# A layer of block products on one core: three of seven products accumulated on one PSUM bank, with half weight units and another order at the turns

## The chip, the cores and the metric

One Trainium2 chip, one core. The metric is device time in microseconds of one execution. The kernel before takes 1847.15 us in the median of three runs (1845.55 to 1848.17).

## What is computed

One layer of a decoder trunk with two gated feed-forward networks and a mixing stage between them, over 1072 tokens (16 meta tokens, 1024 of a prompt, 32 new ones) of width 1024; a feed-forward network has 2816 inner channels.

```python
def rmsnorm(x, g):
    y = xf * lax.rsqrt(jnp.mean(xf * xf, axis=-1, keepdims=True) + EPS)
    return (y * g)
def swiglu(x, wg, wu, wd):
    return (jax.nn.silu(x @ wg) * (x @ wu)) @ wd

x = x + 0.5 * swiglu(rmsnorm(x, g1), w1g, w1u, w1d)
h = rmsnorm(x, gm)
z = h @ w_in + b_in
u = z[..., :C] * sigmoid(z[..., C:2*C])          # then causal conv of width 31, LayerNorm, silu -> c
p_in = z[..., 2*C:]                               # then trailing means over 2/4/8/16 tokens, linear map -> q
x = x + concat([c, q]) @ w_out + b_out
x = x + 0.5 * swiglu(rmsnorm(x, g2), w2g, w2u, w2d)
y = rmsnorm(x, gf)
```

Everything is float32. The outputs are y for prompt and new tokens and the last inputs of convolution and pooling.

## The kernel before, in words

**Numbers and pieces.** Each float32 operand is split into a high part (a cast, by ScalarE, L140) and a low part (source minus high part, L141, by VectorE, or by GpSimd for weights); a product is then three matmuls per 128 input channels: high by high, high by low, low by high (`mul`, L126 to L137; the matmul itself is L123). The tokens stand in three pieces X1, X2, X3 of 358 columns (the first two are padded a little), with channels on the partitions: X1 and X2 go through the first feed-forward network together (the first fast pass), X3 alone (the plain pass); in the second network X1 goes alone and X2 with X3.

**Weights.** A unit is 128 output channels by 1024 input channels or the like, 512 KB. `take` (L159 to L163) gives a loaded unit and issues the load of later ones on SP's queue, into `wraw` with four buffers. `half_unit` (L165 to L169) turns half a unit into `wh` and `wl`, six buffers each.

**Fast passes.** For two pieces, a block of 256 output channels by 1024 input channels is a 2 x 2 product of quarters and is computed with seven products m1 to m7 instead of eight (`block_steps`, L489 to L523). Each product has twelve matmuls of 358 columns and an accumulation bank of its own. VectorE makes four sums of weight quarters per block (L505 to L508). The operands (b11, b21, t1, t2, t3, t4, b22) are made ahead from the two normed pieces. `fast_pair` (L527 to L564) adds the products up: u1 = m1 (a ScalarE copy, L557), u1 + m2, u1 + m6, + m7, + m5 and so on, seven VectorE additions a block, all at L535. The results go to `sink`: a silu by ScalarE and a product by VectorE for the gate and up blocks, and casts and splits for the hidden operands (`group_sink`, L643 to L684; there `hid`, `dt1`, `dt4`, `db22`, `xb`, `cc` are hidden operands, their differences and scratch for them). A block pair p stands in the order gate block, down product of an earlier pair, up block. Four groups of pairs make up a pass; at a group's end the down products of a whole group follow.

**Order.** Matmuls keep the order in which the program emits them. On the other engines a scheduler orders instructions by its own estimates, so how the new program runs on an engine is not told by the diff alone. Background tasks (generators: norms, operands, the mixing stage) are stepped in a queue between the products, and `yield LAG` makes a task wait for that much matmul work (358/2400 a matmul).

**The start** (`Start`, L309 to L427). The first pair's products are made plainly, as the blocks of normed operands aren't there: eight products (c, j), c the piece, j over two gate and two up units, with the norm applied to the results. `norms(c)` makes reciprocal square roots: VectorE iterates, then multiplies an identity by them (`diag`, L206), and TensorE spreads them by a matmul on `ones`; ScalarE copies the result to `nr` (L215).

**Turns.** `to_second_piece` closes the first fast pass, launches `h1b` (the normed X3, split into `smt`) and finishes it. `to_last` launches `s2` (`fast_operands`, L271 to L307: square sums of X2 and X3, then for four k the seven operands of the second fast pass).

## Time and profile before

| | us |
|---|---|
| median of three runs | 1847.15 |
| the profiled execution | 1845.23 |
| its span, first to last instruction | 1843.5 |
| TensorE busy | 1747.4 (95%) |
| VectorE (DVE) busy | 1400.9 (76%) |
| GpSimd (POOL) busy | 1154.1 (63%) |
| ScalarE (ACT) busy | 761.2 (41%) |

The mean granted TensorE clock is 0.973 of full speed. The page's chain of work that ended last is TensorE's for 72% of the span and DVE's for 18%. PE is TensorE's matmuls, SP the engine that issues the loads. "x" counts instructions; a group is one line, engine and operation with its operands.

### The profile page before, as it was taken

To read this page: it belongs to the slowest core of one execution; us is meant where nothing else is said; L and a number is where in the kernel's file an instruction comes from. 1 tells how busy PE (TensorE), PEld (TensorE's weight loads), DVE (VectorE), ACT (ScalarE), POOL (GpSimd) and SP (SyncE) were. 2 spreads that over 40 slices of the span, in tenths; PEclk is the share of its full clock that TensorE was granted. 3 is DMA by queue.
4 is the path that set the end of the run, shared out by engine and by line. 5 is a ranking of instruction groups with operands and counts; after the bars stand their busy time and mean duration, and the time that the engine had idled before them with its cause. 6 is when DMAs were issued, how large, how long until landed. Compare 5 with 4: busy or idle time off the path is not lost.

```text
span 1843.5 us, 29182 instructions
## 1 busy us (share of the span) xinstructions
PE 1747.4 (95%) x10486; PEld 1726.9 (94%) x10486; DVE 1400.9 (76%) x2621; ACT 761.2 (41%) x1482; POOL 1154.1 (63%) x894
## 2 busy tenths in 40 slices
PE   8699999999899999999999999999799999999997
PEld 7699999999799999999999999999699899989997
DVE  8979797989746696898235888537878888797965
ACT  6434444444424324434235433535453434434344
POOL 6576766667635336667246658665577676766683
PEclk9799999999999999999999999999899999999998
DMA  6022222222243223343224493443233222222222
GB/s 204 24 74 78 78 69 69 79 73 95 97 91 119 76 70 101 129 135 118 69 93 136 120 139 127 137 137 120 87 92 94 74 70 69 82 77 72 69 92 87
DMA packets 74560, 176.17 MB, mean 96 GB/s; under 512 B 23728, under 2 KB 30128, under 8 KB 74416
## 3 DMA queue, kind: packets, MB, share of 16 engines
q1 hardware_dynamic: 74416, 174.31, 31.3%
q8 instruction: 83, 1.36, 0.3%
q14 instruction: 61, 0.50, 0.1%
HBM read 169.13 MB, written 5.15 MB: 95 GB/s over the span
## 4 chain that ended last, share of the span: by engine, by line
PE 72%; DVE 18%; issue 5%; DMA 3%; POOL 2%; ACT 1%; SPq 0%; DVEq 0%; POOLq 0%; ACTq 0%
PE acc L123 72%; DMA wraw<-in_wf 3%; POOL wl L141 2%; DVE acc L245 2%; DVE acc L535 1%; DVE wraw L506 1%; DVE tmp L535 1%; DVE acc L779 1%; DVE tmp L245 1%; DVE tmp L657 1%; DVE wraw L507 1%; DVE sx L505 0%; DVE x L456 0%; DVE dt4l L141 0%; DVE xk L245 0%
## 5 line engine op out<-in xcount | busy, mean ns | idle before, releaser
L141 POOL TENSOR_TENSOR wl<-wraw,wh 128x512 fp32r<-128x512 f32 x740 | 996.3, 1358 | 598.2 <-ACT wh L140 567.6
L140 ACT CAST wh<-wraw 128x512 fp32r<-128x512 f32 x740 | 453.9, 620 | 687.9 <-PE acc L123 465.6
L123 PE MATMUL acc<-smt,wh 128*128 128x358 f32 x1024 | 252.8, 328 | 4.5 <-DVE mixl L141 2.2
L123 PEld LDWEIGHTS acc<-smt,wh 128*128 128x128 f32 x1024 | 181.8, 190 | 5.8 <-DVE mixl L141 2.5
L779 DVE SCALAR_TENSOR_TENSOR acc<-ub,vecs,acc 128x340 f32<-128x340 f32 (+2 forms) x348 | 183.7, 573 | 2.7
L123 PE MATMUL acc<-mixlt,wh 128*128 128x340 f32 x704 | 167.0, 321 | 4.9 <-DVE smt L141 2.4
L123 PE MATMUL acc<-smt,wl 128*128 128x358 f32 x512 | 167.8, 328 | 0.0
L456 DVE SCALAR_TENSOR_TENSOR x<-acc,x 128x358 f32<-128x358 f32 (+1 forms) x240 | 119.5, 518 | 38.8 <-PE acc L123 38.1
L583 DVE SCALAR_TENSOR_TENSOR x<-acc,x 128x358 f32<-128x358 f32 x320 | 144.9, 518 | 0.2 <-PE acc L123 0.2
L123 PEld LDWEIGHTS acc<-mixlt,wh 128*128 128x128 f32 x704 | 121.9, 190 | 6.0 <-DVE smt L141 2.7
L535 DVE TENSOR_TENSOR acc<-tmp,acc 128x358 f32<-128x358 f32 x168 | 85.3, 527 | 51.3 <-PE acc L123 45.8
L141 POOL TENSOR_TENSOR wl<-sx,wh 128x512 fp32r<-128x512 f32 x58 | 86.0, 1484 | 49.1 <-ACT wh L140 46.8
L123 PE MATMUL acc<-mixlt,wl 128*128 128x340 f32 x352 | 112.8, 320 | 0.8 <-POOL wl L141 0.8
L123 PEld LDWEIGHTS acc<-smt,wl 128*128 128x128 f32 x512 | 96.9, 189 | 0.0
L505 DVE TENSOR_TENSOR sx<-wraw 128x512 f32<-128x512 f32 x58 | 62.4, 1076 | 38.5 <-DMA wraw<-in_wf 38.3
L507 DVE TENSOR_TENSOR wraw<-sx,wraw 128x512 f32<-128x512 f32 x58 | 78.7, 1357 | 9.8 <-POOL wl L141 9.7
L123 PE MATMUL acc<-mixh,wh 128*128 128x356 f32 (+1 forms) x320 | 79.9, 330 | 4.7 <-DVE mixl L141 2.7
L123 PE MATMUL acc<-mixl,wh 128*128 128x356 f32 (+1 forms) x320 | 79.1, 329 | 0.0
L123 PE MATMUL acc<-mixh,wl 128*128 128x356 f32 (+1 forms) x320 | 79.0, 329 | 0.0
L123 PE MATMUL acc<-xb,wh 128*128 128x358 f32 x256 | 65.9, 339 | 13.6 <-DVE tmp L535 9.6
L535 DVE TENSOR_TENSOR tmp<-tmp,acc 128x358 f32<-128x358 f32 x126 | 65.4, 519 | 13.2 <-PE acc L123 11.4
L482 DVE TENSOR_TENSOR acc<-acc,tmp 128x358 f32<-128x358 f32 (+1 forms) x44 | 23.2, 526 | 64.6 <-PE acc L123 51.2
(284 smaller groups left out, 4873.5 us busy)
## 6 DMA issues: line engine op xcount, KB each, us to landing
wraw<-in_wf SPq DMA_DIRECT2D x239, 512.0 KB, 3.3
wraw<-in_wf SPq DMA_DIRECT2D x66, 256.0 KB, 3.1
wraw<-in_win SPq DMA_DIRECT2D x24, 512.0 KB, 3.3
wraw<-in_wout SPq DMA_DIRECT2D x16, 512.0 KB, 3.3
x<-in_xt SPq DMA_DIRECT2D x8, 179.0 KB, 5.2
x<-in_xt SPq DMA_DIRECT2D x1, 1432.0 KB, 8.5
x<-in_xt SPq DMA_DIRECT2D x8, 178.0 KB, 4.6
out_yt<-tmp SPq DMA_DIRECT2D x8, 170.0 KB, 2.6
```

The lines of the kernel that those rows point to most:

```text
L123: tc.keep_in_program_order(nc.tensor.matmul(acc, lhs, rhs, start=start, stop=stop))
L140: nc.scalar.copy(hi, src)
L141: (engine or nc.vector).tensor_tensor(lo, src, hi, ALU.subtract)
L245: nc.vector.scalar_tensor_tensor(t, X(k, piece), col(gain, k), r, ALU.mult, ALU.mult)
L456: nc.vector.scalar_tensor_tensor(X(m, piece), acc, 0.5, X(m, piece), ALU.mult, ALU.add)
L482: nc.vector.tensor_tensor(acc, acc, box["s"], ALU.mult)
L505: nc.vector.tensor_tensor(s1, r1[:, :KH], r1[:, KH:], ALU.add)
L506: nc.vector.tensor_tensor(r1[:, :KH], r0[:, :KH], r1[:, :KH], ALU.subtract)
L507: nc.vector.tensor_tensor(r0[:, :KH], s1, r0[:, :KH], ALU.subtract)
L535: nc.vector.tensor_tensor(t, s, acc, ALU.add)
L583: nc.vector.scalar_tensor_tensor(to, acc, 0.5 * sign, to, ALU.mult, ALU.add)
L779: nc.vector.scalar_tensor_tensor(to, src, w, part, ALU.mult, ALU.add)
```

## The change

Five edits go together.

1. `chained` takes the place of `product` in 40 of 42 blocks: M6, M7 and M4 accumulate on M1's bank, in the order m1, m2, m6, m5, m7, m3, m4. After M1, M6 and M7 ScalarE copies the bank's state to `tmp` (km1, km6, km7); VectorE adds four times a block. The first pair after the start (`loose`) keeps the old form.
2. Weights come in half units: `wraw` tiles of 256 KB, eight of them, five loaded ahead.
3. X3's square sum is taken in the middle of the first fast pass from a copy that is loaded again into `tmp`, piece by piece.
4. `h1b` isn't finished at once, and the last pair's down product stands ahead of the plain pass; X2's norm for the second fast pass is launched with the mixing stage, and `fast_operands` makes its operands in another order, with one accumulation bank and three `tmp`.
5. The start makes the second norm after product (1, 0), and reads norms from the accumulation bank where it read them from `nr`; `outputs` writes to the products' own banks.

```diff
+LAG5 = 20.0
+LAG6 = 4.0
...
-R_BUFS = 4
+R_BUFS = 8
+AHEAD = 5
...
-        tc.keep_in_program_order(nc.tensor.matmul(acc, lhs, rhs, start=start, stop=stop))
+    def matmul(acc, lhs, rhs, start, stop, more=False):
+        tc.keep_in_program_order(nc.tensor.matmul(acc, lhs, rhs, start=start, stop=stop, skip_group_check=more))
...
-        return const.tile([P, KD, P], F32, name="wraw", tag="wraw", bufs=R_BUFS)
+        return const.tile([P, KH, P], F32, name="wraw", tag="wraw", bufs=R_BUFS)
...
-        fetch(2)
+        fetch(AHEAD)
...
+    def early_rms(piece, out):
+        a, b = piece
+        s = const.tile([P, N], F32, name="ns", tag="ns")[:, : b - a]
+        part = accum()[:, : b - a]
+        for k in range(KD):
+            t = temp()[:, : b - a]
+            nc.sync.dma_start(t, xt[:, k, a - PAD : b - PAD])
+            yield
+            if k == 0:
+                nc.scalar.activation(part, t, AF.Square)
+            else:
+                nc.scalar.activation(t, t, AF.Square)
+                nc.vector.tensor_tensor(s if k == KD - 1 else part, part, t, ALU.add)
+            yield
+        yield LAG5
+        out[piece] = yield from rsqrt(s, 1.0 / D, EPS, lag=LAG5)
...
-        yield from rms(p0, st)
-        yield from rms(p1, st)
+        for piece in pieces:
+            if piece not in st:
+                yield from rms(piece, st)
+        sub = nc.vector.tensor_tensor
         for k in range(KH):
-            b11, b21, b12, b22, t3 = (temp()[:, :n] for _ in range(5))
+            b11, b22, b21 = (temp()[:, :n] for _ in range(3))
+            t = accum()[:, :n]
             scaled(b11, p0, k, gain, st[p0])
+            scaled(b22, p1, KH + k, gain, st[p1])
+            yield
+            put("b11", k, b11)
+            put("b22", k, b22)
+            yield
+            scaled(t, p1, k, gain, st[p1])
+            t3 = temp()[:, :n]
+            sub(t3, b22, t, ALU.subtract)
+            sub(t, t, b11, ALU.subtract)
+            yield
+            put("t1", k, t)
+            put("t3", k, t3)
             scaled(b21, p0, KH + k, gain, st[p0])
             yield
-            put("b11", k, b11)
+            sub(t, b22, t, ALU.subtract)
+            put("t2", k, t)
             put("b21", k, b21)
             yield
-            scaled(b12, p1, k, gain, st[p1])
-            scaled(b22, p1, KH + k, gain, st[p1])
-            yield
-            nc.vector.tensor_tensor(t3, b22, b12, ALU.subtract)
-            nc.vector.tensor_tensor(b12, b12, b11, ALU.subtract)
-            yield
-            put("t1", k, b12)
-            put("t3", k, t3)
-            put("b22", k, b22)
-            yield
-            nc.vector.tensor_tensor(b22, b22, b12, ALU.subtract)
-            put("t2", k, b22)
-            yield
-            nc.vector.tensor_tensor(b21, b21, b22, ALU.subtract)
-            put("t4", k, b21)
-            yield
+            sub(t, b21, t, ALU.subtract)
+            put("t4", k, t)
+            yield LAG6
...
-                self.outputs(0)
+                self.norms(1)
+                self.gate(0)
+                self.outputs(0, 0)
+                self.outputs(0, 1)
                 self.first_blocks()
             elif (c, j) == (1, 0):
                 self.norms(1)
-            elif (c, j) == (1, 2):
-                self.norms(1)
+            elif (c, j) == (1, 1):
+                self.gate(1)
                 self.differences()
-            elif (c, j) == (1, 3):
-                self.outputs(1)
-                self.last_blocks()
-                rest_of_start()
-        def outputs(self, c):
+            elif c == 1:
+                self.outputs(1, j - 2)
+                if j == 3:
+                    self.last_blocks()
+                    rest_of_start()
...
+        def gate(self, c):
             r = self.st[c]
             for i in range(2):
-                t = pools["fast"].tile([P, self.n], F32, name="cc", tag="cc", bufs=4)
+                t = self.gates[i] = pools["fast"].tile([P, self.n], F32, name="cc", tag="cc", bufs=4)
                 nc.vector.tensor_tensor(t, self.accs[c, "g", i], r, ALU.mult)
                 nc.scalar.activation(t, t, AF.Silu)
-                nc.vector.tensor_tensor(t, t, r, ALU.mult)
-                nc.vector.tensor_tensor(t, self.accs[c, "u", i], t, ALU.mult)
-                if i not in self.hid:
-                    fa1_places(0)
-                split(self.hid[i][0][c], self.hid[i][1][c], t)
+                nc.vector.tensor_tensor(t, t, self.inbank[c], ALU.mult)
+        def outputs(self, c, i):
+            acc = self.accs[c, "u", i]
+            nc.vector.tensor_tensor(acc, acc, self.gates[i], ALU.mult)
+            if i not in self.hid:
+                fa1_places(0)
+            split(self.hid[i][0][c], self.hid[i][1][c], acc)
...
+        def kept(acc):
+            t = temp()[:, :n]
+            nc.scalar.copy(t, acc)
+            return t
+        def chained(name, w):
+            ops = get()[OPERAND_OF[name]]
+            on = name in ("m6", "m7", "m4")
+            acc = st["m1"] if on else accum()[:, :n]
+            block_product(acc, w, ops, not on)
+            if name in ("m1", "m6", "m7"):
+                st["m1"], st["k" + name] = acc, kept(acc)
+            elif name == "m2":
+                sink(0, 0, add(st["km1"], acc, acc))
+            elif name == "m5":
+                st["m5"] = acc
+            elif name == "m4":
+                sink(1, 0, acc)
+            else:
+                sink(0, 1, add(st["u4"], acc, acc))
+            if name == "m7":
+                st["u4"] = add(st["km6"], st["m5"], st["km6"])
+                sink(1, 1, add(st["km7"], st["m5"], st["m5"]))
...
-        return block_steps(src0, src1, product)
+        return block_steps(src0, src1, product if loose else chained)
...
+    CHAINED = ("m12", "m6", "m5", "m7", "m3", "m4")
...
-                put_blocks(g)
+                put_blocks(g, CHAINED)
...
+            elif p == 4 and first:
+                do(launch, "r1b", early_rms(FFN1_B, r1b))
...
-        launch("r1b", rms(FFN1_B, r1b))
...
-        finish("h1b")
     do(to_second_piece)
     put_down(fa1_d[PAIRS - 2])
+    put_down(fa1_d[PAIRS - 1])
     def to_first_mixing():
         close_pool("fast")
@@ -1129,7 +1197,7 @@
         open_pool("low", "right")
         open_mix()
-    plain_pass(fb1, fb1_d, fa1_d[PAIRS - 1], {
+    plain_pass(fb1, fb1_d, [], {
...
+        launch("s2", fast_operands(FFN2_B, "g2", box["s2"], r2b))
...
+            lambda: do(launch, "r2", rms(FFN2_B[0], r2b))],
```

In the order of instructions of each engine, three places change most. (New line numbers: L144 and L145 are the cast and the split L140 and L141; L576 the copy; L601 the addition L535; L266 is L245; L490 is L456; L516 is L482; a number behind a name tells apart tiles.)

ScalarE at the end of the first group of the first fast pass: before,

```order
L140 CAST wh<-wraw 128x512
L140 CAST hid1h<-acc 128x358
L140 CAST wh<-wraw 128x512
L140 CAST db22h_1404<-acc 128x358
L140 CAST wh<-wraw 128x512
L140 CAST dt4h_1448<-cc 128x358
L140 CAST hid2l<-tmp 128x358
L140 CAST wh<-wraw 128x512
L140 CAST hid0h<-acc 128x358
L557 COPY tmp<-acc 128x358
L140 CAST wh<-wraw 128x512
```

and now,

```order
L144 CAST wh<-wraw 128x512
L144 CAST xb<-cc 128x358
L144 CAST wh<-wraw 128x512
L144 CAST hid1h<-acc 128x358
L144 CAST hid0h<-acc 128x358
L144 CAST wh<-wraw 128x512
L576 COPY tmp<-acc 128x358
L144 CAST dt4h_1486<-cc 128x358
L144 CAST dt4h_1487<-cc 128x358
L727 ACTIVATE cc<-acc 128x358
L144 CAST wh<-wraw 128x512
L576 COPY tmp<-acc 128x358
```

The copy of M1 of the next block (the first L576 row; L557 before) stands in both behind the two `hid` casts of the finished group; now it has M6 of its block behind it, and the next two copies follow.

VectorE at the turn to the plain pass, where `smt` is made from X3: before,

```order
L141 TENSOR_TENSOR hid2l<-acc,hid2h 128x358
L637 TENSOR_TENSOR acc<-acc,cc 128x358
L245 SCALAR_TENSOR_TENSOR acc<-x_4804,vecs,nr 128x358
L141 TENSOR_TENSOR smt<-acc,smt 128x358 x4
L245 SCALAR_TENSOR_TENSOR acc<-x_4804,vecs,nr 128x358
L141 TENSOR_TENSOR hid1l<-acc,hid1h 128x358
L141 TENSOR_TENSOR smt<-acc,smt 128x358
L245 SCALAR_TENSOR_TENSOR acc<-x_4804,vecs,nr 128x358
L141 TENSOR_TENSOR db22l_5206<-acc,db22h_5204 128x358
L141 TENSOR_TENSOR smt<-acc,smt 128x358 x3
L456 SCALAR_TENSOR_TENSOR x_61<-acc,x_61 128x358
L456 SCALAR_TENSOR_TENSOR x_62<-acc,x_62 128x358
```

and now,

```order
L490 SCALAR_TENSOR_TENSOR x_61<-acc,x_61 128x358
L490 SCALAR_TENSOR_TENSOR x_62<-acc,x_62 128x358
L266 SCALAR_TENSOR_TENSOR acc<-x_4948,vecs,nr 128x358 x2
L490 SCALAR_TENSOR_TENSOR x_61<-acc,x_61 128x358
L490 SCALAR_TENSOR_TENSOR x_62<-acc,x_62 128x358
L266 SCALAR_TENSOR_TENSOR acc<-x_4948,vecs,nr 128x358
L145 TENSOR_TENSOR smt<-acc,smt 128x358 x2
L266 SCALAR_TENSOR_TENSOR acc<-x_4948,vecs,nr 128x358
L490 SCALAR_TENSOR_TENSOR x_61<-acc,x_61 128x358
L490 SCALAR_TENSOR_TENSOR x_62<-acc,x_62 128x358
L266 SCALAR_TENSOR_TENSOR acc<-x_4948,vecs,nr 128x358
L145 TENSOR_TENSOR smt<-acc,smt 128x358
```

The products of X3 by its norm (L245, now L266) and the `smt` splits ran in one piece; now the additions of the down product to x (L490) stand between.

VectorE at the turn to the second fast pass, from the diagonal (`diag`) on: before,

```order
L141 TENSOR_TENSOR b11l<-tmp,b11h 128x358
L141 TENSOR_TENSOR b21l<-tmp,b21h 128x358
L295 TENSOR_TENSOR tmp<-tmp 128x358
L141 TENSOR_TENSOR b22l<-tmp,b22h 128x358
L296 TENSOR_TENSOR tmp<-tmp 128x358
L482 TENSOR_TENSOR acc<-acc,tmp 128x340
L141 TENSOR_TENSOR t3l<-tmp,t3h 128x358
L302 TENSOR_TENSOR tmp<-tmp 128x358
L245 SCALAR_TENSOR_TENSOR tmp<-x_62,vecs,nr 128x358 x2
L141 TENSOR_TENSOR t1l<-tmp,t1h 128x358
L245 SCALAR_TENSOR_TENSOR tmp<-x_4804,vecs,nr 128x358
L141 TENSOR_TENSOR hid0l<-acc,hid0h 128x340
```

and now,

```order
L266 SCALAR_TENSOR_TENSOR tmp<-x_62,vecs,nr 128x358
L145 TENSOR_TENSOR b11l<-tmp,b11h 128x358
L516 TENSOR_TENSOR acc<-acc,tmp 128x340
L145 TENSOR_TENSOR hid1l<-acc,hid1h 128x340
L266 SCALAR_TENSOR_TENSOR tmp<-x_4948,vecs,nr 128x358
L266 SCALAR_TENSOR_TENSOR acc<-x_4948,vecs,nr 128x358 x2
L319 TENSOR_TENSOR tmp<-tmp,acc 128x358
L145 TENSOR_TENSOR b22l<-tmp,b22h 128x358
L320 TENSOR_TENSOR acc<-acc,tmp 128x358
L266 SCALAR_TENSOR_TENSOR tmp<-x_62,vecs,nr 128x358
L145 TENSOR_TENSOR t3l<-tmp,t3h 128x358
L145 TENSOR_TENSOR t1l<-acc,t1h 128x358
```

A `hid` split of the plain pass comes after three operations of the operands' making instead of after some fifteen, and t1's and t2's source is an `acc` tile in place of a `tmp`.

## Rows read from the trace of the kernel before

**Rows 1.** The page: span, and each engine's busy time.

```profile
span 1843.5 us, 29182 instructions
PE 1747.4 (95%) x10486; PEld 1726.9 (94%) x10486; DVE 1400.9 (76%) x2621; ACT 761.2 (41%) x1482; POOL 1154.1 (63%) x894
```

**Rows 2.** Table by stretch: start:end length, busy time of each engine, PEclk, DMA share, GB/s.

```profile
0.00:125.00 125.00, 100.23 (x537) 95.93 (x538) 104.82 (x181) 62.24 (x127) 81.99 (x69) 0.89 0.32 106
125.00:450.00 325.00, 317.38 (x1890) 314.06 (x1889) 286.24 (x477) 132.50 (x255) 219.53 (x161) 0.98 0.23 76
480.00:525.00 45.00, 38.81 (x223) 38.36 (x222) 27.56 (x51) 14.99 (x31) 18.48 (x14) 0.92 0.22 71
1262.00:1345.00 83.00, 68.29 (x416) 66.46 (x416) 67.93 (x113) 37.12 (x76) 43.26 (x31) 0.92 0.26 89
1440.00:1800.00 360.00, 349.96 (x2086) 344.83 (x2085) 308.42 (x515) 148.12 (x284) 247.68 (x183) 0.99 0.24 78
```

**Rows 3.** The same table for a stretch at full clock and for the first 35 us.

```profile
350.00:400.00 50.00, 50.00 (x306) 50.00 (x305) 39.59 (x70) 19.83 (x37) 35.66 (x26) 1.00 0.25 83
0.00:35.00 35.00, 29.24 (x148) 26.70 (x149) 26.26 (x54) 26.75 (x54) 19.63 (x20) 0.90 0.73 243
```

**Rows 4.** TensorE's waits (total, times, longest), 125 to 475 and 1345 to 1800.

```profile
PE acc L123 <- DVE tmp L535: 6.0, 6, 1.4
PE acc L123 <- DVE ns L235: 2.1, 1, 2.1
...
PE acc L123 <- DVE tmp L535: 6.6, 8, 1.4
```

**Rows 5.** Timeline around one group end: DVE and PE (start, duration, [idle before]).

```profile
1439.24 1.70 DVE L141 TENSOR_TENSOR xb<-cc,xb 128x358 fp32r<-128x358 f32 x1 [0.56 <-ACT xb L140]
...
1461.75 0.60 PE L123 MATMUL acc<-xb,wh 128*128 128x358 f32 x2 [0.45 <-DVE cc L681]
1464.00 0.59 PE L123 MATMUL acc<-xb,wh 128*128 128x358 f32 x2 [0.99 <-ACT cc L661]
1466.65 0.60 PE L123 MATMUL acc<-xb,wh 128*128 128x358 f32 x2 [1.42 <-DVE tmp L535]
1468.39 0.44 PE L123 MATMUL acc<-hid0h,wh 128*128 128x358 f32 x1 [0.48 <-DVE tmp L535]
```

**Rows 6.** Additions and weight casts (the page's groups) and the copy L557 (its line).

```profile
L140 ACT CAST wh<-wraw 128x512 fp32r<-128x512 f32 x740 | 453.9, 620 | 687.9 <-PE acc L123 465.6
L535 DVE TENSOR_TENSOR acc<-tmp,acc 128x358 f32<-128x358 f32 x168 | 85.3, 527 | 51.3 <-PE acc L123 45.8
L535 DVE TENSOR_TENSOR tmp<-tmp,acc 128x358 f32<-128x358 f32 x126 | 65.4, 519 | 13.2 <-PE acc L123 11.4
...
L557 ACT COPY tmp<-acc x42: 448/459/483, 71.7 to 1783.8; 128x358 f32<-128x358 f32 x42
```

**Rows 7.** Timeline at the turn to the plain pass: DVE and PE.

```profile
492.87 5.74 DVE L245 SCALAR_TENSOR_TENSOR acc<-x,vecs,nr 128x358 f32<-128x358 f32 x5
...
504.47 1.11 PE L123 MATMUL acc<-dt1h,wh 128*128 128x358 f32 x2 [6.19 <-DVE smt L141]
```

**Rows 8.** Timeline at the turn to the second fast pass: DVE and PE.

```profile
1314.50 1.59 DVE L141 TENSOR_TENSOR t4l<-tmp,t4h 128x358 fp32r<-128x358 f32 x1
...
1318.70 0.65 PE L123 MATMUL acc<-hid2h,wh 128*128 128x340 f32 x1 [10.18 <-ACT hid2h L140]
1321.11 0.65 PE L123 MATMUL acc<-hid2l,wh 128*128 128x340 f32 x1 [1.75 <-DVE hid2l L141]
...
1322.89 0.50 DVE L456 SCALAR_TENSOR_TENSOR x<-acc,x 128x340 f32<-128x340 f32 x1
```

**Rows 9.** Timeline of the start: PE.

```profile
51.55 1.65 PE L123 MATMUL acc<-diag,ones 128*128 128x128 f32 x6 [7.74 <-DVE diag L206]
...
66.45 0.67 PE L123 MATMUL acc<-b11h,wh 128*128 128x358 f32 x1 [6.07 <-DVE cc L383]
```

**Rows 10.** The page's DMA issues of weights: KB each, median us to landing.

```profile
wraw<-in_wf SPq DMA_DIRECT2D x239, 512.0 KB, 3.3
wraw<-in_wf SPq DMA_DIRECT2D x66, 256.0 KB, 3.1
wraw<-in_win SPq DMA_DIRECT2D x24, 512.0 KB, 3.3
wraw<-in_wout SPq DMA_DIRECT2D x16, 512.0 KB, 3.3
```

More of the change, by code (lines that the diff above doesn't have):

```diff
@@ L135, in mul @@
                     moving = rhs[c] if isinstance(rhs, list) else rhs[:, at : at + n]
-                    matmul(acc, lhs, moving, start and i == 0 and j == 0, stop and i == last and j == 2)
+                    matmul(acc, lhs, moving, start and i == 0 and j == 0, stop and i == last and j == 2,
+                           more)
                     at += n
@@ L169, in half_unit, with unit @@
         return wh, wl
-    def unit(raw):
-        return half_unit(raw[:, :KH]), half_unit(raw[:, KH:])
+    def unit():
+        return half_unit(take()), half_unit(take())
     def both_parts(w, k):
@@ L182, in blocks, with rsqrt @@
         return [min(at, n - P) for at in range(0, n, P)]
-    def rsqrt(src, scale, add, out=None, copied=True):
+    def rsqrt(src, scale, add, out=None, copied=True, lag=LAG2):
         n = src.shape[-1]
@@ L347, in norms @@
             if c not in self.steps:
-                self.steps[c] = rsqrt(self.sums[c], 1.0 / D, EPS)
+                self.steps[c] = rsqrt(self.sums[c], 1.0 / D, EPS, self.out[c])
                 next(self.steps[c])
@@ L351, in norms @@
                 self.st[c] = whole(self.steps[c])
+                self.inbank[c] = self.out[c]["psum"]
         def after(self, c, j):
@@ L456, in use @@
                         nc.vector.scalar_tensor_tensor(X(m, piece), acc, 0.5, X(m, piece), ALU.mult, ALU.add)
-            out.append(("step", [source], lambda: unit(take()), use, False))
+            out.append(("step", [source], lambda: unit(), use, False))
         return out
     def plain(src, use):
-        return ("step", [[(0, src)]], lambda: unit(take()), use, False)
+        return ("step", [[(0, src)]], lambda: unit(), use, False)
     def plain_ffn(wsrc, piece, get):
@@ L493, in make0 @@
         def make0():
-            st["r0"] = take()
-            return unit(st["r0"])
+            st["r0"] = take(), take()
+            return tuple(half_unit(r) for r in st["r0"])
         def use0(w):
@@ L553, in product @@
             ops = get()[OPERAND_OF[name]]
-            mul([acc], [(w[0][:, k], w[1][:, k], ops[0][:, k], ops[1][:, k]) for k in range(KH)])
+            block_product(acc, w, ops)
             if name == "m1":
@@ L593, in twist, with fast_ffn @@
             yield
-    def fast_ffn(wsrc, pieces, free, get, hid):
+    def fast_ffn(wsrc, pieces, free, get, hid, loose):
         n = N
@@ L1210, in use @@
                     between(m)
-        return ("step", raws, lambda: (unit(take()), unit(take())), use, False)
+        return ("step", raws, lambda: (unit(), unit()), use, False)
     def between(m):
@@ L1230, in trunk @@
     for p in steps:
-        raw_list.extend(p[1])
-    raw_list[0] = [(at, raw_list[0][0][1][:, at * P : (at + KH) * P]) for at in (0, KH)]
+        for _, src in sum(p[1], []):
+            raw_list.extend(src[:, at : at + KH * P] for at in range(0, src.shape[-1], KH * P))
     nc.sync.dma_start(vecs, vec)
     start.load(0, 0)
-    fetch(1)
+    fetch(2)
     for k in range(1, KD):
         start.load(0, k)
-    fetch(2)
+    fetch(4)
     for k in range(KD):
```

56 lines of the change are left out of this document (28 added, 28 removed).

## The prediction

> **What bounds the kernel now.** The first view is the page's list of engines: TensorE works 95% of the span, and it is the only engine near full; ScalarE works 41% of it [rows 1]. So a change pays only where it removes TensorE's losses. The second view is the table by stretch, from which I read two losses: the time in which TensorE does nothing (length less PE busy) and the time in which it works at less than the full granted clock ((1 - PEclk) x length). In 125 to 450 these are 7.6 + 6.5 = 14.1 us, in 1440 to 1800 they are 10.0 + 3.6 = 13.6 us, in 480 to 525 6.2 + 3.6 = 9.8 us, and in 1262 to 1345 14.7 + 6.6 = 21.3 us [rows 2]. The first two stretches are the two fast passes (blocks in seven products), the third is the turn from the first fast pass to the plain pass, the fourth the turn from the plain pass to the second fast pass. At full clock 306 matmuls take 50.00 us, so a matmul takes 163 ns and a product of twelve 1.96 us [rows 3]; that is the unit in which I measure every delay below.
>
> The third view tells what TensorE waits for. In the fast stretches nearly all of it is the DVE addition at L535: 6.0 us in 6 waits in the first, 6.6 us in 8 in the second; one wait of 2.1 us on the sum of squares of X3 (`ns`) comes beside them [rows 4]. The timeline of one group end shows how: four waits of 0.45, 0.99, 1.42 and 0.48 us, 3.3 us together, follow each other, while DVE works without a gap [rows 5].
>
> **The chained blocks.** Forty blocks give up three of seven additions each (7 in `settle` and `product`; 4 in `chained`): 120 operations of 0.53 us [rows 6] that start 0.44 us apart, some 53 us of DVE work. TensorE does no more and no fewer matmuls. DVE is not the bound on average, so this is worth only what it moves in the group ends. There two blocks stand behind each other, so 6 x 0.44 = 2.6 us of the 3.3 us of wait go. If the 12.6 us of waits on L535 go, and with them their share of the clock loss (12.6 of 17.6 us idle, so 7.2 of 10.1 us), it is 19.8 us; the half units and the freed banks (4 instead of 7 per block) can add a little and the stretching of DVE's operations beside GpSimd's, such as the 1.70 us of an `xb` split [rows 5], can take some back. I take **-18 us**; bounds -5 (only the longest wait of each group end shortens) and -25.
>
> Against it stand the new copies. M6 may not write on M1's bank before ScalarE has copied it, M7 not before the copy of M6, M4 not before that of M7. A copy takes 0.46 us and a cast 0.62 us [rows 6]. In the new order of ScalarE (first place shown above) one weight cast stands ahead of most copies. With six operand buffers, that cast (six products ahead) waits for the buffer which the product to be copied has just freed, so the copy is there about 0.62 + 0.46 = 1.08 us after its product's end, and another product of 1.96 us lies between (M2, M5, M3): no wait. At the eight group ends the order is worse: the copy of the first M1 stands behind both `hid` casts, which wait for some ten DVE operations after M3 of the group, and behind a cast for which M2 must have ended. So M6 waits at least 1.08 us from M2's end, more where one of those operations is stretched. I take 1.4 us, **+11 us** for eight; bounds 0 (the new stall only takes the place of the old ones) and +28 (3.5 us each: two splits stretched from 0.53 to 1.70 us on top of 1.08).
>
> **X3's statistics early.** They are computed in the middle of the pass from a copy read again, instead of at its end. The wait of 2.1 us [rows 4] goes: **-2 us** (0 to -4 with the clock). The price is eight more transfers on SP's queue that wait for a free `tmp` and have weight loads behind them; five half units are ahead there, 5 x 1.96 = 9.8 us of cover. If the cover were gone, the next thing late would be a weight cast; bound +4 us.
>
> **h1b interleaved.** Before, the whole second operand is made ahead of two downs: TensorE stands 6.19 us for `smt` splits, because the banks of those norms are held while DVE works off five L245 of 1.15 us and the splits [rows 7]. In the new order (second place) the 96 matmuls of each down, 15.7 us at 163 ns, lie between, and DVE alternates between L490 and L266. The 6.19 us go, and part of the 3.6 us of clock: **-8 us** of 9.8; bounds -4 and -9.8. What is late next is an `smt` split at the plain pass's first unit.
>
> **s2 shortened.** At the last turn TensorE waits 10.18 us for `hid2h` and 1.75 us for `hid2l`, since ScalarE and DVE work first through the fast operands of the second pass; a split of two SBUF operands took 1.59 us there, an operation with one PSUM operand 0.50 us [rows 8]. The change gives t1, t2 and t4 a PSUM tile, which makes about half of its 60 operations of the second kind; it takes X2's square sum out of this place; and it sets a pause of 4 units of the program's clock (358/2400 a matmul, so 27 matmuls) between the four k, so that `hid` operations come sooner (third place). Sixty operations lose some 30 x 0.5 = 15 us of DVE time, more than the 11.9 us of waits. **-16 us** of the stretch's 21.3; bounds -8 (only the clock and the small wait) and -20.
>
> **Start.** The second norm's diagonal is now awaited one product of each kind earlier. Before, TensorE waits 7.74 us for it and 6.07 us for the gate product [rows 9]. Two products of 24 matmuls, 7.8 us at 163 ns, move behind the first wait: it gets longer by up to that, and the second has that much more cover. **0 us**; bounds -6 (the second wait gone) and +8 (nothing won back).
>
> **Half units.** Transfers of 256 KB took 3.1 us where those of 512 KB took 3.3 us [rows 10]; the count of weight transfers goes from 345 to 624. In the first 35 us, where all queues are loaded, 243 GB/s were moved [rows 3], more than one transfer at a time gives (256 KB in 3.1 us are 85 GB/s), so transfers overlap, and the 71 to 106 GB/s of the stretches [rows 2] are below it. Nothing for itself: **0 us** (their use is in the -18); bounds 0 and the rival below. The Trainium skill, "DMA: Bandwidth & Descriptors", section Bandwidth, speaks against this edit: transfers should be gathered to 1 MiB or more, and 64 KB ones reach only 32% of the peak. By that rule the edit costs time where loads are the bound (rival 5). The trace agrees that the fixed part is most of a transfer (3.1 us against 3.3 us for twice the bytes).
>
> **Sum**, against the profiled execution's 1845.2 us (its span is 1843.5): -18 + 11 - 2 - 8 - 16 + 0 = -33, so 1812 us. The median of the runs is 1.9 us above that execution; so 1814 us is the forecast for the median.
>
> **Rivals.**
> 1. *No new wait.* The ScalarE copies are on time at group ends too. For it: ScalarE is idle 59% of the time. Against: the order itself puts `hid` casts ahead. 1814 - 11 = 1803 us.
> 2. *The wait only changes its name.* At group ends M6 waits as long for the copy as the downs waited for L535; the fast passes win nothing. For it: the DVE chain that ends in `hid` is the same. 1845.2 - 26 + 1.9 = 1821 us.
> 3. *The turns keep their waits.* h1b and s2 are late at the next place, since the operands are still needed by the plain pass's first unit and by the second fast pass's first block. Only the fast passes and X3 win: 1845.2 - 9 + 1.9 = 1838 us. Against: in both turns DVE's work gets shorter or has 31 us of matmuls beside it.
> 4. *Slower: every chained step waits.* If a second cast stands ahead of the copy, or the one ahead waits for the next product's buffer (ten copies of the new order stand so), each of the 120 steps M6, M7 and M4 waits for a cast and a copy: 120 x 1.08 = 130 us. With the -44 of the other terms that gives 1845.2 + 86 + 1.9 = 1933 us. It decides from 44 / 120 = 0.37 us a step, that is when the copy is there later than 1.96 + 0.37 = 2.3 us after its product. Against: one cast ahead for 110 of 120 copies, so 1.08 us.
> 5. *Slower: the queue.* If half units went one at a time, 624 x 3.1 = 1934 us would be more than the span, and the kernel would be bound by loads at about 1936 us. Against: the overlap at the start. For it stands the Trainium skill's rule on gathering transfers, named above.
>
> **How the numbers follow.** Forecast 0.42, rival 1 0.20, rival 2 0.17, rival 3 0.09, rival 4 0.07, rival 5 0.02, and 0.03 for gains and losses that cancel. A measurement of this kernel tells about 0.2% (3.7 us) from no change. Faster by more than that are the forecast and the first three rivals, less a little of the third: 0.86; within it 0.05; slower 0.09. The range reaches from below rival 1 (the fast passes' bound of -25 and s2's of -20 would give 11 us less than 1803, of which I take most) to rival 3: 1793 to 1838 us.
>
> **What would show it.** Right: 174 additions at L601 instead of 294 at L535 and 120 copies at L576; waits of TensorE on DVE's `tmp` in the fast stretches down from 12.6 us to under 4; waits on ScalarE's L576 copies eight times of 1 to 2 us, and nowhere else; no wait on `ns` near 470 us; the 6.19 and 10.18 us waits gone; a longer wait for the second diagonal before 50 us and a shorter one after it; landing times of 256 KB near 3 us. Wrong: a mean granted clock not above 0.973, since then idle time only moved; waits on copies in every block (rival 4); DVE idle for `wraw` transfers in the middle of the passes (rival 5); or a wait for `smt` or b/t operands at the first unit after either turn (rival 3).

## The result and the profile after

The changed kernel takes 1823.5 us (median of 4 runs, 1815.1 to 1826.8) against 1846.4 us (4 runs): a ratio of 0.987 with the interval [0.983, 0.991], so 1.3% or 23 us faster. The forecast was 1814 us, 33 us faster. The profiled execution took 1826.8 us, the longest of the four, with a span of 1824.9 against 1843.5 us; its mean granted clock is 0.976 (0.973 before). One execution of a variant below (e_s2) took 9589.5 us and is left out of that variant's median.

First the page of the changed kernel: span and engines, and the groups that answer to [rows 6].

```profile
span 1824.9 us, 29625 instructions
PE 1742.4 (95%) x10486; PEld 1728.0 (95%) x10486; DVE 1325.1 (73%) x2501; ACT 799.8 (44%) x1562; POOL 1138.7 (62%) x894
...
L601 DVE TENSOR_TENSOR acc<-tmp,acc 128x358 f32<-128x358 f32 x128 | 66.6, 529 | 93.1 <-PE acc L126 78.4
L126 PE MATMUL acc<-t2h,wh 128*128 128x358 f32 x184 | 65.1, 354 | 19.8 <-ACT tmp L576 19.8
wraw<-in_wf SPq DMA_DIRECT2D x544, 256.0 KB, 2.9
```

DVE has 120 operations less and works 76 us less. The loads of 256 KB land in 2.9 us. But a new group stands there: TensorE's first matmul of M6 (`t2h`) waits 19.8 us in all for ScalarE's copies.

The table by stretch, with its bounds moved so that each stretch covers the same place of the program as in [rows 2]; the counts of matmuls differ, as less time is lost in a stretch of about the same length (start:end length, busy times, PEclk, DMA share, GB/s):

```profile
0.00:125.00 125.00, 103.02 (x546) 99.79 (x547) 93.73 (x184) 62.73 (x128) 81.28 (x70) 0.86 0.34 109
125.00:450.00 325.00, 314.69 (x1883) 313.22 (x1882) 271.40 (x452) 150.56 (x291) 214.21 (x159) 0.98 0.26 81
475.00:520.00 45.00, 44.68 (x269) 43.84 (x268) 27.67 (x54) 17.77 (x35) 22.33 (x17) 1.00 0.28 86
1245.00:1327.00 82.00, 77.27 (x482) 76.33 (x481) 55.40 (x101) 41.59 (x84) 47.79 (x38) 0.98 0.36 109
1425.00:1785.00 360.00, 349.41 (x2091) 347.64 (x2090) 286.18 (x464) 165.12 (x320) 242.16 (x182) 0.99 0.24 76
```

Idle time and clock loss added as in the prediction, the two turns lose 0.3 us (9.8 before) and 4.7 + 1.6 = 6.4 us (21.3 before): 24 us won, as forecast. The start loses 22.0 + 17.5 = 39.5 us where it lost 24.8 + 13.8 = 38.5: nothing. The two fast passes lose 10.3 + 6.5 = 16.8 and 10.6 + 3.6 = 14.2 us, together 31 us where they lost 27.7: they got no better. Here is what TensorE waits for in these two stretches (125 to 450 and 1425 to 1785), against [rows 4]:

```profile
PE acc L126 <- ACT tmp L576: 10.3, 5, 2.6
...
PE acc L126 <- ACT tmp L576: 10.6, 5, 2.6
```

Every wait on a DVE addition is gone, and one on a copy stands in its place. The first group's end on ScalarE and TensorE shows it (timeline: start, duration, engine, [idle before]):

```profile
146.90 0.62 ACT L144 CAST wh<-wraw 128x512 fp32r<-128x512 f32 x1
147.82 0.46 ACT L144 CAST hid1h<-acc 128x358 fp32r<-128x358 f32 x1 [0.31 <-DVE acc L723]
149.74 0.46 ACT L144 CAST hid0h<-acc 128x358 fp32r<-128x358 f32 x1 [1.46 <-DVE acc L723]
150.09 0.62 ACT L144 CAST wh<-wraw 128x512 fp32r<-128x512 f32 x1
150.61 0.46 ACT L576 COPY tmp<-acc 128x358 f32<-128x358 f32 x1
...
151.13 0.67 PE L126 MATMUL acc<-t2h,wh 128*128 128x358 f32 x1 [2.59 <-ACT tmp L576]
```

and DVE ahead of it:

```profile
147.26 0.53 DVE L723 TENSOR_TENSOR acc<-acc,dt1l 128x358 f32<-128x358 f32 x1
147.70 1.56 DVE L145 TENSOR_TENSOR xb<-cc,xb 128x358 fp32r<-128x358 f32 x1
149.18 0.53 DVE L723 TENSOR_TENSOR acc<-acc,dt1l 128x358 f32<-128x358 f32 x1
```

Read it from the bottom up. M6 could start at 148.5 us. It waits for the copy of M1, which ScalarE could have made at 146.6 us, when M1's last matmul ended; but in ScalarE's order two `hid` casts and two weight casts stand ahead, the second `hid` cast waits for DVE's subtraction at 149.18, and that one stands behind an `xb` split of 1.56 us, three times its length elsewhere. This is the place and the chain that the prediction named; it took 2.6 us where 1.4 were put down. It is 2.6 us at seven of the eight group ends; at the eighth M6 waits 0.95 us. By the Trainium skill, "SBUF — State Buffer", section Who interferes with whom, a DVE operation with both inputs in SBUF contends with a GpSimd operation that reads SBUF; the trace agrees, since the split of `cc` and `xb` took 1.56 us while GpSimd split weights (146.25 to 148.87 us), and subtractions from `acc` on either side took 0.53 us.

Most of these waits are followed by a lower granted clock. A stretch of 25 us from such a wait on (table by stretch):

```profile
150.00:175.00 25.00, 23.87 (x136) 23.87 (x137) 21.69 (x36) 11.82 (x24) 15.21 (x11) 0.93 0.16 52
```

and the same stretch in the fastest variant below (e_order):

```profile
150.00:175.00 25.00, 24.71 (x150) 24.13 (x148) 24.97 (x42) 9.98 (x19) 17.74 (x13) 1.00 0.21 65
```

The 0.93 is a mean over 25 us, in which some 1.7 us are given away: right behind the wait, matmuls start 0.30 us apart, at the lower of the clock's two levels (1.2 GHz), and later 0.16 us apart. Five of the seven waits of 2.6 us were followed by such a fall; after those before 1435.8 and 1521.6 us the same view shows 1.00. Against the kernel before, no clock is lost on top: its fast passes lost the same 6.5 + 3.6 us with waits of 1.4 us at most.

### The profile page after: what moved, and what is told of

Same layout as the page of the kernel before. It is cut to its first block, busy times and chain, and to the rows that moved or that the text cites. A ratio compares the mean times of both kernels' runs of the same rounds, so it can differ in the third digit from the quotient of the medians.

```text
span 1824.9 us, 29625 instructions
## 1 busy us (share of the span) xinstructions
PE 1742.4 (95%) x10486; PEld 1728.0 (95%) x10486; DVE 1325.1 (73%) x2501; ACT 799.8 (44%) x1562; POOL 1138.7 (62%) x894
## 3 DMA queue, kind: packets, MB, share of 16 engines
q1 hardware_dynamic: 115744, 175.80, 33.1%
## 4 chain that ended last, share of the span: by engine, by line
PE 81%; DVE 13%; issue 2%; ACT 2%; DMA 1%; POOL 0%; SPq 0%; DVEq 0%; ACTq 0%; POOLq 0%
PE acc L126 81%; DVE acc L266 2%; DMA wraw<-in_wf 1%; DVE acc L845 1%; DVE xb L145 1%; DVE tmp L266 1%; DVE sx L541 1%; DVE x L490 1%; DVE wraw L544 1%; ACT wh L144 1%; DVE acc L601 1%; DVE pr L863 1%; DVE acc L731 0%; DVE acc L723 0%; DVE cc L731 0%
## 5 line engine op out<-in xcount | busy, mean ns | idle before, releaser
L145 POOL TENSOR_TENSOR wl<-wraw,wh 128x512 fp32r<-128x512 f32 x740 | 986.8, 1341 | 627.2 <-ACT wh L144 609.3
L144 ACT CAST wh<-wraw 128x512 fp32r<-128x512 f32 x740 | 456.4, 621 | 728.2 <-PE acc L126 523.1
L649 DVE SCALAR_TENSOR_TENSOR x<-acc,x 128x358 f32<-128x358 f32 x320 | 148.6, 518 | 19.4 <-PE acc L126 19.2
L490 DVE SCALAR_TENSOR_TENSOR x<-acc,x 128x358 f32<-128x358 f32 (+1 forms) x240 | 119.7, 517 | 35.9 <-PE acc L126 35.1
L601 DVE TENSOR_TENSOR acc<-tmp,acc 128x358 f32<-128x358 f32 x128 | 66.6, 529 | 93.1 <-PE acc L126 78.4
L145 POOL TENSOR_TENSOR wl<-sx,wh 128x512 fp32r<-128x512 f32 x58 | 81.6, 1408 | 24.8 <-ACT wh L144 24.6
L541 DVE TENSOR_TENSOR sx<-wraw 128x512 f32<-128x512 f32 x58 | 72.8, 1255 | 16.4 <-DMA wraw<-in_wf 16.0
L126 PE MATMUL acc<-t2h,wh 128*128 128x358 f32 x184 | 65.1, 354 | 19.8 <-ACT tmp L576 19.8
L126 PE MATMUL acc<-b11h,wh 128*128 128x358 f32 x184 | 62.1, 338 | 10.8 <-ACT wh L144 10.8
L542 DVE TENSOR_TENSOR wraw<-wraw 128x512 f32<-128x512 f32 x58 | 71.5, 1233 | 1.1
L516 DVE TENSOR_TENSOR acc<-acc,tmp 128x358 f32<-128x358 f32 (+1 forms) x44 | 23.2, 526 | 65.8 <-PE acc L126 53.5
```

The lines of the kernel that those rows point to most:

```text
L126: tc.keep_in_program_order(nc.tensor.matmul(acc, lhs, rhs, start=start, stop=stop, skip_group_check=more))
L144: nc.scalar.copy(hi, src)
L145: (engine or nc.vector).tensor_tensor(lo, src, hi, ALU.subtract)
L490: nc.vector.scalar_tensor_tensor(X(m, piece), acc, 0.5, X(m, piece), ALU.mult, ALU.add)
L516: nc.vector.tensor_tensor(acc, acc, box["s"], ALU.mult)
L541: nc.vector.tensor_tensor(s1, a21, a22, ALU.add)
```

## Experiments

The theory after the result: the two turns gave all of the gain, and chaining only exchanged the wait on an addition for a wait on a copy. Twelve kernels took the edits apart. Each is compared with the kernel before, run on the same chip (1846.6 to 1848.9 us). The changed kernel's own interval is 7 us wide to either side, so that a difference to it below some 7 us is read from the traces.

| kernel | median us | ratio to before |
|---|---|---|
| changed kernel | 1823.5 | 0.987 [0.983, 0.991] |
| unchained, old order of products (e_nochain) | 1807.2 | 0.978 [0.976, 0.980] |
| unchained, new order of products (e_order) | 1797.4 | 0.972 [0.971, 0.974] |
| chained, copy ahead of the hid casts (e_defer) | 1817.1 | 0.983 [0.982, 0.984] |
| chained, M1's copy by DVE at group ends (e_dvecopy) | 1845.6 | 1.000 [0.999, 1.001] |
| chained but for the group ends (e_looseend) | 1821.9 | 0.987 [0.984, 0.989] |
| full units again (e_full) | 1835.4 | 0.994 [0.993, 0.996] |
| old s2 (e_s2) | 1832.9 | 0.992 [0.990, 0.994] |
| old h1b (e_h1b) | 1829.2 | 0.989 [0.988, 0.991] |
| old start (e_start) | 1828.9 | 0.991 [0.989, 0.992] |
| unchained, old order, start's differences earlier (e_best) | 1801.2 | 0.975 [0.973, 0.976] |
| before + chaining alone (e_onlychain) | 1849.7 | 1.001 [1.000, 1.002] |
| before + half units alone (e_half) | 1833.9 | 0.992 [0.991, 0.993] |

### Chaining undone

```diff
-    fa1, fa1_d, fa1_places = fast_ffn(wf1, FFN1_A, 2, lambda: box["s1"]["ops"], hid_a1, lambda p: p == 1)
+    fa1, fa1_d, fa1_places = fast_ffn(wf1, FFN1_A, 2, lambda: box["s1"]["ops"], hid_a1, lambda p: True)
...
-    fb2, fb2_d, _ = fast_ffn(wf2, FFN2_B, 0, got("s2", "ops"), hid_b2, lambda p: False)
+    fb2, fb2_d, _ = fast_ffn(wf2, FFN2_B, 0, got("s2", "ops"), hid_b2, lambda p: True)
-    CHAINED = ("m12", "m6", "m5", "m7", "m3", "m4")
+    CHAINED = USUAL
```

> The changed kernel with no block chained: all 42 blocks add seven times on DVE on banks of their own, in the old order of products; the other four edits stay. Theory A (the fast passes only exchanged one wait for another; the gain is that of the two turns): 1823 us, within 5 of the changed kernel; the 23.5 us of waits on ScalarE's copies are gone and 12 to 18 us of waits on DVE's additions and on casts are back. Theory B (chaining pays the 18 us of the prediction and another edit takes them back): about 1841 us.

It came out at 1807 us, outside both: 16 us *faster* than the changed kernel. Not only the waits on copies are gone; of the waits on additions (12.6 us in [rows 4]) only 1.6 us came back. From TensorE's waits in the fast stretches (125 to 450, 1425 to 1765), 10.8 us in all, most of them on silus (L727, L699) by ScalarE:

```profile
PE acc L126 <- ACT cc L727: 2.1, 3, 1.2
PE acc L126 <- DVE tmp L601: 1.3, 1, 1.3
...
PE acc L126 <- ACT cc L727: 3.7, 3, 1.2
...
PE acc L126 <- DVE tmp L601: 0.3, 1, 0.3
```

So something else in the change had already removed the waits on additions, and theory A in its first form falls: chaining does not exchange one wait for another in this kernel, it adds one.

### Chaining alone, and half units alone

The first puts `chained`, its order of products and the matmul flag into the kernel before; the second puts the changed `wraw`, `fetch`, `take`, `unit` and `sums` there.

> The kernel before with the chained blocks alone (full units, old turns, old start). Theory A: no change, 1846 us within 5; waits on the copies of M1 at the eight group ends of 2 to 3 us each, waits on additions gone. Theory B: about 1828 us.

> The kernel before with half units alone (no chaining, old turns, old start). By the undone edits so far the half units give about 12 us, and the unchained fast passes lose almost nothing in the changed kernel. Theory H (half units take the place of the waits on additions at group ends by themselves): 1828 to 1836 us, waits of TensorE on additions in the two fast passes down from 12.6 us to under 5. Rival (they only pay with the new turns and start): 1843 to 1848 us.

Chaining alone gave 1.001: no gain, as theory A said. The waits on additions are gone here too, and M6 waits 22.7 us for copies, in the group of its matmuls (idle before, and what ended it):

```profile
L123 PE MATMUL acc<-t2h,wh 128*128 128x358 f32 x184 | 65.9, 358 | 23.4 <-ACT tmp L540 22.7 <-ACT nr L215 0.5
```

Half units alone gave 15 us (0.992), as theory H said. TensorE's waits in the first fast stretch, 125 to 450 (new line numbers: L663 and L635 are the silus L661 and L633), and both fast stretches in the table:

```profile
PE acc L124 <- ACT cc L663: 3.7, 3, 1.2
PE acc L124 <- ACT cc L635: 1.2, 1, 1.2
...
125.00:450.00 325.00, 319.70 (x1929) 316.24 (x1928) 292.91 (x485) 137.08 (x264) 224.77 (x164) 1.00 0.24 78
1440.00:1790.00 350.00, 344.39 (x2079) 340.98 (x2078) 308.05 (x512) 146.25 (x282) 246.44 (x181) 1.00 0.24 77
```

No wait on an addition is left there, nor in the second stretch; 9.8 us of waits on silus stand in the two, where the kernel before had 3.7. Idle time falls from 17.6 to 10.9 us, and the 10.1 us of clock loss are gone: the larger part of the 15 us is clock. Half units do by themselves what the prediction gave to chaining.

### Full units in the changed kernel

```diff
-R_BUFS = 8
-AHEAD = 5
+R_BUFS = 4
+AHEAD = 4
...
-        return const.tile([P, KH, P], F32, name="wraw", tag="wraw", bufs=R_BUFS)
+        return const.tile([P, KD, P], F32, name="wraw", tag="wraw", bufs=R_BUFS)
...
-            fetched.append(raw)
+            fetched.append(raw[:, :KH])
+            fetched.append(raw[:, KH:])
```

> The changed kernel with weight loads of 512 KB again (four buffers, up to two and a half units ahead); all else stays. If the size of the loads is worth nothing: 1823 us within 5. If half units cost (more transfers on the queue): 1815 us or less. If they helped to feed the sums of weight quarters: 1830 us or more, DVE idle for loads before the sums at some 38 us instead of 16.

Full units cost 12 us (0.994 against 0.987). VectorE's first sum of weight quarters shows where, from 125 to 450, in the changed kernel and with full units (busy, mean ns | idle before, and its cause):

```profile
L541 DVE TENSOR_TENSOR sx<-wraw 128x512 f32<-128x512 f32 x22 | 32.0, 1452 | 3.3 <-DMA wraw<-in_wf 3.1
```

```profile
L544 DVE TENSOR_TENSOR sx<-wraw 128x512 f32<-128x512 f32 x22 | 21.2, 965 | 19.0 <-DMA wraw<-in_wf 18.9
```

DVE stands 19 us in front of loads with full units and 3 us with half ones, and the additions and splits that follow on DVE start that much later. TensorE's waits on copies in the two fast stretches grow from 20.9 to 26.5 us.

What the loads themselves wait for is seen on SP's queue, in the same stretch with full units and then with half ones:

```profile
SPq L159 <- POOL wl L145: 296.1, 44, 16.9
```

```profile
SPq L157 <- DVE wraw L544: 174.1, 23, 10.5
SPq L157 <- POOL wl L145: 107.9, 60, 5.6
```

The queue waits nearly all the time for a buffer to come free; a full unit holds its buffer until GpSimd has split both halves. The landing itself took only 0.4 us longer (3.3 against 2.9 us). So the smaller load, the earlier release of half a buffer and the lead (four half units at least against five) come together in this edit; no run took them apart.

Twice as many transfers cost nothing that the traces show, beyond a busy share of the DMA engines of 33.1% instead of 31.5%, and rival 5 falls: with 624 of them, the kernel is faster. The Trainium skill's rule of gathering transfers to 1 MiB ("DMA: Bandwidth & Descriptors", section Bandwidth) names a share of the peak bandwidth as its aim; followed here, it would have kept the full units. The measurement decides against it: the DMA engines are busy for 33% of the span only.

### The order of products

Unchained as above, with one line more:

```diff
-    CHAINED = USUAL
+    CHAINED = ("m12", "m6", "m5", "m7", "m3", "m4")
```

> The changed kernel unchained, but with the products in the order of the chained blocks (m5 ahead of m7, m3 ahead of m4). Theory A (chaining costs by the wait of M6 for its copy): 1807 us within 4, as unchained in the old order. Rival (the other order of products costs it, since results for the silu and the hidden operands come later): 1818 us or more.

1797 us, below both: the new order of products, without the shared bank, is worth 10 us, and this is the fastest kernel of the study, 2.8% below the kernel before. At equal order, chaining costs 26 us, which the fast passes account for (31 us lost there with it, 3.8 us and no clock without). The waits of TensorE in 125 to 450 and 1425 to 1760, all of them:

```profile
PE acc L126 <- ACT cc L727: 1.0, 3, 0.6
PE acc L126 <- ACT wh L144: 0.5, 1, 0.5
PE acc L126 <- ACT cc L699: 0.2, 1, 0.2
...
PE acc L126 <- ACT cc L727: 0.6, 3, 0.2
PE acc L126 <- ACT hid1h L144: 0.5, 1, 0.5
PE acc L126 <- ACT cc L699: 0.2, 1, 0.2
```

3.0 us of waits remain (3.8 us idle, at a clock of 1.00), where the kernel before lost 17.6 us idle and 10 us of clock. What the order does is seen on DVE at the first group's end. In the old order (e_nochain) the second hidden operand's split runs at 154.07 us, 10.3 us after the next block's M1 began (143.76 us):

```profile
151.77 1.78 DVE L543 TENSOR_TENSOR wraw<-sx,wraw 128x512 f32<-128x512 f32 x1
153.47 0.68 DVE L541 TENSOR_TENSOR sx<-wraw 128x512 f32<-128x512 f32 x1
154.07 0.52 DVE L145 TENSOR_TENSOR hid0l<-acc,hid0h 128x358 fp32r<-128x358 f32 x1
```

and in the new order at 147.87 us, 4.9 us after it (142.94 us):

```profile
147.43 0.52 DVE L145 TENSOR_TENSOR xb<-cc,xb 128x358 fp32r<-128x358 f32 x1
147.87 0.52 DVE L145 TENSOR_TENSOR hid0l<-acc,hid0h 128x358 fp32r<-128x358 f32 x1
```

With M3 ahead of M4, the result from which `hid` is made is there one product earlier, and DVE's chain ends before the weight sums come between. That this alone is the 10 us is argued from these rows; no run moved M3 and M5 separately.

### The copy moved, three ways

e_defer hands the up block's last two results to their sink only after the next block's M2; e_dvecopy copies M1 with DVE in the eight gate blocks behind a group's end; e_looseend leaves these eight unchained, in the old order. Their main lines, in this order:

```diff
+        def give(*where):
+            if hold:
+                state["late"].append((sink, where))
+            else:
+                sink(*where)
...
+                for put_late, where in state["late"]:
+                    put_late(*where)
...
+            if vector:
+                nc.vector.tensor_copy(t, acc)
...
-            pairs.append((fast_pair(wsrc[4 * p], wsrc[4 * p + 1], get, n, gate, loose(p)),
+            pairs.append((fast_pair(wsrc[4 * p], wsrc[4 * p + 1], get, n, gate, loose(p) or p - 2 in GROUPS),
```

> The changed kernel, chained, but with the last two results of the up block at a group's end handed to their sink after the next block's M2, which puts the copy of M1 ahead of both hid casts on ScalarE; nothing else moves by itself. Theory A (the place behind the hid casts is the reason): the eight waits of M6 of some 2.6 us fall to 1 us or less, and the kernel comes to 1800 to 1810 us. Rival (the DVE chain bounds the place, as when DVE made the copy): the wait moves to xb, hid or dt operands: 1820 us within 5.

> The changed kernel with the copy of M1 made by DVE instead of ScalarE in the eight gate blocks behind a group's end. Theory A (the copy stands behind hid casts on ScalarE's queue, that is the whole wait): the waits of M6 shrink from 2.6 us to under 0.5 each, 18 us of idle time and some clock less: 1803 to 1811 us. Rival (the DVE chain behind the group bounds those places whoever copies): the wait moves to xb and hid operands a few us later: 1820 us within 5.

> The changed kernel with the eight gate blocks behind a group's end left unchained (own banks, old order), the other 32 chained. Theory A with the DVE additions as the reason of the old waits: the M6 waits go, and since 24 fewer of the saved additions stand in those blocks, half of the old 3.3 us per group end comes back: 1813 us, 1808 to 1820. Rival (the place loses some 2.5 us whatever is done): 1823 us within 5.

In e_defer the copy of M1 stands ahead of the `hid` casts, and M6 waits no more. But M7 and M4 now do, as their group rows show:

```profile
L126 PE MATMUL acc<-t2h,wh 128*128 128x358 f32 x184 | 61.5, 334 | 0.0
L126 PE MATMUL acc<-t4h,wh 128*128 128x358 f32 x168 | 57.2, 341 | 11.3 <-ACT tmp L576 11.3
L126 PE MATMUL acc<-t3h,wh 128*128 128x358 f32 x168 | 55.8, 332 | 6.2 <-ACT tmp L576 6.2
```

The longest of them, M4's 5.18 us at 246 us, is for a copy of M7 that stands behind a square of X3's early statistics, which waited for DVE:

```profile
245.24 0.50 ACT L259 ACTIVATE tmp<-tmp 128x358 f32<-128x358 f32 x1 [3.74 <-DVE acc L260]
245.65 0.44 ACT L576 COPY tmp<-acc 128x358 f32<-128x358 f32 x1
```

So theory A was right on the place (no wait of M6) and wrong that the place was all of it: 1817 us is above its range, and 6 us below the changed kernel, no more than the runs can tell. In the trace the waits on copies fall from 23.6 to 17.5 us. An instruction ahead of a copy on ScalarE that waits, as this square did for DVE, stops TensorE.

With DVE as the copier it is worse, 1846 us, and both expectations (a gain, or 1820 us) fell: M6 waits 4.5 us at each group's end, eight times, since on DVE the copy stands behind the whole chain of the finished group. PE and DVE at the first end:

```profile
151.27 0.67 PE L126 MATMUL acc<-t2h,wh 128*128 128x358 f32 x1 [4.48 <-DVE tmp L577]
...
150.69 0.53 DVE L577 COPY tmp<-acc 128x358 f32<-128x358 f32 x1
```

e_looseend, 1822 us, came within the interval of the changed kernel: the waits of M6 are gone, and in the fast stretches 11.9 us of waits on additions and 6.7 us on copies for M4 stand in their place. The mixture of old and new blocks wins nothing, as its rival said. Why additions are waited for again there, and not in the wholly unchained kernel, was not followed up; the order of products differs between them.

### The turns and the start undone

e_s2 takes the old `fast_operands` and drops the launch of X2's norm, e_h1b finishes `h1b` at once, and e_start takes the old `norms`, `after`, `outputs` and `block`. The lines of the first two beside those functions:

```diff
-            lambda: do(launch, "r2", rms(FFN2_B[0], r2b))],
...
+        finish("h1b")
-    put_down(fa1_d[PAIRS - 1])
-    plain_pass(fb1, fb1_d, [], {
+    plain_pass(fb1, fb1_d, fa1_d[PAIRS - 1], {
```

> The changed kernel with the old operands' order of the second fast pass and X2's square sum back in it. If the s2 edit gave the 15 us that the stretch of the turn lost less: 1838 us, with the wait of some 10 us for hid2h back. If the gain of that turn came from the half units or from the earlier diagonal: 1823 us within 5, no such wait.

> The changed kernel with h1b finished at once and the last pair's down product back in the plain pass. If interleaving gave the 9.5 us that this turn lost less: 1833 us, with a wait of about 6 us behind the smt splits. If X3's early statistics alone removed that wait: 1823 us within 5.

> The changed kernel with the old start (second diagonal after product (1, 2), norms read from the copy). The two starts lose the same in the trace, 16 to 17 us of waits each: 1823 us within 5. Rival: the wait of 9.3 us on a weight cast at 70.9 us in the new start is a pure loss: 1815 us.

The old s2 costs some 9 us by the medians, and brings back the waits of [rows 8] to a tenth of a microsecond (1245 to 1340); that stretch loses 14.7 + 6.6 = 21.3 us in its trace, as before the change, which is 15 us more than in the changed kernel:

```profile
PE acc L126 <- ACT hid2h L144: 10.2, 1, 10.2
PE acc L126 <- DVE hid2l L145: 1.7, 1, 1.7
```

The old h1b costs some 4 to 6 us, not 9.5, which is within what the runs can tell: 2.8 us of waits for `smt` come back, not the 6.19 us of [rows 7]. The kernel before with chaining alone, without X3's early statistics, shows the same 2.8 us (470 to 530, e_h1b and e_onlychain):

```profile
PE acc L126 <- DVE smt L145: 2.8, 2, 2.3
...
PE acc L123 <- DVE smt L141: 2.8, 2, 2.3
```

With half units alone the wait stays at 6.2 us. So chained blocks, with their fewer additions and their order, are enough to take the other 3.4 us; whether the early statistics would do it too is open, since no run took them out alone.

The old start's waits are up to 7.7 us on `diag` and 6.2 us on the gate, as in [rows 9], against 6.5 and 9.3 us in the new one. Its median, 1829 us, is 5 us higher, at the edge of what the runs can tell and just outside the 1823 us within 5; its first 125 us lose 24.9 + 15.0 = 39.9 us in the trace, against 39.5 in the changed kernel.

### An earlier start

In e_best, products unchained in the old order, the first gate and the start's differences are emitted ahead of product (1, 1).

```diff
                 self.norms(1)
-            elif (c, j) == (1, 1):
-                self.gate(1)
+                self.gate(1, 0)
                 self.differences()
+            elif (c, j) == (1, 1):
+                self.gate(1, 1)
```

> The changed kernel unchained, with the differences of the start emitted before product (1, 1) and the second gate after them. DVE stands idle 3.9 us for product (1, 1) before the differences in the trace of the changed kernel. If that chain bounds the start: 1802 to 1805 us, 2 to 5 us less than unchained alone. If the products' banks or the gate bound it: 1807 us within 3, or some us more.

1801 us, 6 us below the same kernel without it (0.975 against 0.978): the wait of 9.3 us before the first block became one of 5.2 us, and the first 125 us lose 19.0 + 12.5 = 31.5 us instead of 24.1 + 13.8 = 37.9. It wasn't tried on top of the new order of products.

## Why the prediction was right, and where it failed

- **Direction and range** held: faster, by 23 us of the 33 forecast, near rival 2 (1821 us), which also had the picture right: the fast passes won nothing and the turns gave the gain. Its reason, the DVE chain that ends in `hid`, holds for the chained blocks, whose copy stands behind it; the unchained ones show that it does not bound the fast passes by itself. That the number came near is partly luck: chaining cost 26 us, and half units and the order of products, which the sum did not price apart, gave 12 to 15 and 10 us back.
- **The two turns** were the gain: -8 and -16 us were forecast and -9.5 and -15 us are found in the stretches. The mechanism was right for s2, whose undoing brings both waits back; one figure of its sum, 0.5 us saved an operation, is not what its rows give (1.59 - 0.50 = 1.09 us in [rows 8]). For h1b only part of the 9.5 us is its own: undoing it brings 2.8 us of waits back, and the rest is gone with chaining alone too.
- **X3's statistics**: -2 us were forecast, and the wait on `ns` is gone. Chaining alone left 0.6 us of that wait and half units alone 1.3, so not all of it need be this edit's; no run undid it alone. No cost showed behind its transfers on SP. The cost that did come was not named: in the chained variants the squares stand in front of copies on ScalarE.
- **The start**: 0 us forecast, 1 us lost in the trace. One wait got longer and the other stayed, though it changed its name (from `cc` to a ScalarE cast at 70.9 us).
- **The step that failed is the one on the chained blocks**, -18 and +11. The waits on additions went, but the fast passes won nothing of the -18 us by it: they lost 31 us instead of 27.7. Without any chaining the half units end those waits too (15 us, where the prediction put 0 for them and "a little" within the -18), and the order of products gives 10 us more. The +11 us were right in mechanism and place and mis-sized: 2.6 us instead of 1.4 at seven of eight group ends, 23.6 us of waits on copies in all with M4's 3.8, which were not expected; and the 7.2 us of clock loss that the -18 counted as won stayed. Taken against the best unchained kernel, chaining costs 26 us. The bound given for the +11 was +28.
- **Half units**, 0 us in the sum, are worth 12 to 15 us. I had looked at their cost on the queue and not at what waits for a load: DVE's first sums, which stood idle 38 us for loads in the kernel before and 12 us with half units alone.

## What to carry to other kernels

Accumulating on a bank that another engine must first copy puts that engine's whole queue between two matmuls. Saving 120 operations on an engine that isn't the bound won nothing here, as it came with a wait of another kind; look first at what the late engine itself waits for, here loads of whole units into buffers that came free late. And where an edit brings several things at once, undo them one at a time: here the shared bank cost more than any other part gave.

## What the runs showed that was not expected

- Doubling the number of transfers and halving their size made the kernel 12 to 15 us faster; 256 KB landed in 2.9 us, 512 KB in 3.3 us before.
- Five of seven waits of 2.6 us were followed by a fall of the granted clock, to a mean of 0.93 over 25 us or lower, and two were not. The unchained kernel in the new order, with no wait over 0.6 us in its fast stretches, shows 1.00 there, and so does the one in the old order, with waits of up to 1.3 us.
- Reordering the seven products of a block, with the same matmuls, moved the time by 10 us.
